# A sixth place for raw weights, paid for with the scratch tiles of an MLP's activation sums

## The chip, the cores and the metric

One NeuronCore of a Trainium2 chip runs the whole program. The metric is the device time of one execution in microseconds (us); a lower time is better. Times of a kernel are the median of several runs on a chip; one more execution is taken with the hardware profiler, and all spans, waits and busy times below come from that one.

## The reference

A two-layer decoder trunk on 256 tokens of width 2048, in float32. Layer 0 mixes tokens by differential attention, layer 1 by a Mamba-2 scan; after each mixer stands a squared-ReLU MLP, and it is the two MLPs that the change touches:

```
def sq_relu_mlp(h, w1, w2):
    return jnp.square(jax.nn.relu(h @ w1)) @ w2

for i in range(2):
    h = h + mixer_i(rms_norm(h, mixer_norm[i]))
    h = h + sq_relu_mlp(rms_norm(h, mlp_norm[i]), mlp_w1[i], mlp_w2[i])
```

`w1` is 2048 x 8192, `w2` is 8192 x 2048. Every weight is used once.

## The kernel before, in words

**Weights.** All weights stream from HBM in units of 128 x 1024 float32 (512 KB). A unit is loaded by the queue of SP (line 186) into a tile named `raw`; five places in SBUF hold such tiles in turn, and all stages share them. ScalarE (ACT) then rounds the unit to the fast matmul format (line 158), VectorE (DVE) subtracts to get the rest (line 159), and TensorE (PE) multiplies with both halves. The two halves make a `w` tile, of which there are four. So a unit passes through SP, ACT, DVE and PE, and a place of `raw` is free again when ACT and DVE have read it. SP issues its loads strictly in order: a load whose place is still in use holds up all loads behind it.

**Attention and Mamba stages** use `wide_pair` (lines 169 and 173) and `token_block` (lines 238 and 240): about 2.7 us of matmuls for each unit.

**The MLP.** The hidden width of 8192 is made in eight chunks of 1024. `MLP_KINDS = "sSSSSSSS"`: chunk 0 is made plainly (`blocks`, by `wide_steps`), the others by `seven`, a Strassen-like scheme with seven products of half-size blocks in place of eight. It needs sums of weights, which DVE makes: lines 569, 579, 584 and 600, each on 128 x 1024. It also needs sums of activations: `sum_parts` makes them eight times at the head of each MLP, from two pairs of activation tiles each time. One call is two additions into a tile `a` (line 530), four half-width additions into a tile `asum` (lines 534 to 537), a rounding by ACT (line 540) and a subtraction by DVE (line 541) into `sa`, which the products read. `a` and `asum` are scratch: they share a pair of 2 KB places of their own (tag `relu`) in the MLP's pool.

**Order.** The kernel is Python code that issues instructions; `side` holds generators that are ticked between matmuls, among them `norm_input` (activations of the next stage) and `sums_of` (which calls `sum_parts`). A tile scheduler then settles the order on each engine and which place a tile gets: a tile that finds no free place of its tag is delayed, and other instructions go first. Afterwards each engine runs its list strictly in order.

At the head of an MLP four things meet: the last residual additions of the mixer (line 319, in four pairs, each after a block of PE), the new activations (lines 273 and 274), the eight calls of `sum_parts`, and the first weights. The first two chunks are interleaved (`both(0, 28 / 12)`), so the first `seven` begins while chunk 0 is under way.

Of the kernel before, what the change touches and what calls it, by code (L numbers as in the profile page):

```python
# [12 lines left out]
F32 = mybir.dt.float32  # L13
# [7 lines left out]
P = 128  # L21
T = 256
# [69 lines left out]
def trunk_kernel(ctx: ExitStack, tc: tile.TileContext, x, xt, par, rope, qk, wv, wo, w10, w10s, w20, win, wdt, wout, w11, w11s, w21, out):  # L92
# [5 lines left out]
    wp = ctx.enter_context(tc.tile_pool(name="wp", bufs=1))  # L98
# [81 lines left out]

    def load(src, n=1):

        raw = wp.tile([P, 1024], F32, tag="raw", bufs=5, name="raw")
        w = 1024 // n
        for i in range(n):
            nc.sync.dma_start(out=raw[:, i * w:(i + 1) * w], in_=src[:, i * w:(i + 1) * w])
        return raw
# [4 lines left out]
    def wide_pair(src, b, acts):  # L192

        pp = [bank() for _ in range(2)]
        for s in range(2):
            raw = [load(src[b + t, s]) for t in range(2)]
            w = [split_weights(raw[t]) for t in range(2)]
            for i in range(2):
                for t in range(2):
                    sub_part(w[t], acts, 8 * s, pp[t], i, s == 0, s == 1)  # L200
        return pp

    def wide_steps(src, b, acts, dst):

        pp = bank()
        for s in range(2):
            sub_block(split_weights(load(src[b, s])), acts, 8 * s, pp, s == 0, s == 1)
            yield
        add_sums(dst, [pp])

    def wide_one(src, b, acts):
        pp = bank()
        raw = [load(src[b, s]) for s in range(2)]
        for s in range(2):
            sub_block(split_weights(raw[s]), acts, 8 * s, pp, s == 0, s == 1)
        return pp
# [51 lines left out]
    def x_parts(src, j, gain):  # L268

        t, parts = act_pair()  # L270
        for i in range(2):
            g = pa[:, gain + 2 * j + i:gain + 2 * j + i + 1]
            S.activation(t[:, i, 0, :], src[:, i, :], AF.Identity, scale=g)
            V.scalar_tensor_tensor(out=t[:, i, 1, :], in0=src[:, i, :], scalar=g, in1=t[:, i, 0, :].bitcast(F32),
                                   op0=ALU.mult, op1=ALU.subtract)
        return parts
# [48 lines left out]
    with tc.tile_pool(name="xin", bufs=1) as xp:  # L325
        raw, xf = [], []
        for s in range(2):
            pool = (wp, xp)[s]
            raw.append([pool.tile([P, 1024], F32, tag="raw", bufs=(5, 4)[s], name="raw") for _ in range(4)])
        for g in range(4):  # L330
            for j in range(2):
                xf.append(xp.tile([P, 2, T], F32, tag="xf", bufs=8, name="xf"))
                nc.sync.dma_start(out=xf[-1], in_=x[2 * g + j])
                if j == 0:
                    for b in range(4):
                        c = slice(512 * (g % 2), 512 * (g % 2 + 1))
                        nc.sync.dma_start(out=raw[g // 2][b][:, c], in_=qk[b, g // 2][:, c])
        w = None
        for g in range(4):
            if g % 2 == 0:  # L340
                w = [wp.tile([P, 2, 1024], F32R, tag="w", bufs=4, name="w") for _ in range(4)]
            for j in range(2):
                xs += x_parts(xf[2 * g + j], 2 * g + j, C_MIX0)
            for b in range(4):
                c = slice(512 * (g % 2), 512 * (g % 2 + 1))
                src = raw[g // 2][b][:, c]
                S.copy(out=w[b][:, 0, c], in_=src)
                V.tensor_tensor(out=w[b][:, 1, c], in0=src, in1=w[b][:, 0, c].bitcast(F32), op=ALU.subtract)
                for i in range(2):
                    for k in range(4):  # L350
                        kk = slice(512 * (g % 2) + k * P, 512 * (g % 2) + (k + 1) * P)
                        act = xs[4 * g + k]
                        if i == 0:
                            PE.matmul(first[b], lhsT=w[b][:, 0, kk], rhs=act, start=(g + k == 0), stop=False)
                        else:
                            PE.matmul(first[b][:, 0, :], lhsT=w[b][:, 1, kk], rhs=act[:, 0, :], start=False, stop=(g + k == 6))
# [168 lines left out]

    def sum_parts(pool, x, dst):

        a = pool.tile([P, 2, T], F32, tag="relu", bufs=2, name="a")
        for i in range(2):
            V.tensor_tensor(out=a[:, i, :], in0=x[i][:, 0, :].bitcast(F32), in1=x[i][:, 1, :].bitcast(F32), op=ALU.add)  # L530
        a11, a21, a12, a22 = (a[:, i, t * P:(t + 1) * P] for i in range(2) for t in range(2))
        f = pool.tile([P, 4, P], F32, tag="relu", bufs=2, name="asum")
        yield
        V.tensor_tensor(out=f[:, 0, :], in0=a21, in1=a22, op=ALU.add)
        V.tensor_tensor(out=f[:, 1, :], in0=f[:, 0, :], in1=a11, op=ALU.subtract)
        V.tensor_tensor(out=f[:, 2, :], in0=a11, in1=a21, op=ALU.subtract)
        V.tensor_tensor(out=f[:, 3, :], in0=a12, in1=f[:, 1, :], op=ALU.subtract)
        yield
        sa = pool.tile([P, 2, 4, P], F32R, tag="sa", bufs=8, name="sa")
        S.copy(out=sa[:, 0], in_=f)  # L540
        V.tensor_tensor(out=sa[:, 1], in0=f, in1=sa[:, 0].bitcast(F32), op=ALU.subtract)
        x0, x1 = x
        s1, s2, s3, s4 = ([sa[:, i, n, :] for i in range(2)] for n in range(4))
        dst.append([[x0[:, i, 0:P] for i in range(2)], s4, [x1[:, i, 0:P] for i in range(2)], s1, s3, s2, [x1[:, i, P:T] for i in range(2)]])
        yield
# [64 lines left out]
    def mlp(xs, w1, w1s, w2, pool, after):  # L610
# [3 lines left out]
        def sums_of():  # L614
            for j in range(KT // 2):
                while len(xs) < 2 * j + 2:
                    yield
                yield from sum_parts(pool, xs[2 * j:2 * j + 2], sas)
# [458 lines left out]
```

## Time and profile before

| what | value |
|---|---|
| median of 3 runs | 2450.47 us (2450.01 to 2451.3) |
| the profiled execution | 2449.62 us, its span 2447.9 us |
| PE busy | 2434.1 us, 99% of the span |
| PE weight loads busy | 2038.8 us, 83% |
| DVE busy | 2098.2 us, 86% |
| ACT busy | 1535.6 us, 63% |
| read from HBM | 496.24 MB, 204 GB/s over the span |
| attention | 0 to about 380 us |
| MLP of layer 0 | about 380 to 1070 us |
| Mamba | about 1070 to 1740 us |
| MLP of layer 1 | about 1740 to 2448 us |

The page of the profile lists busy times by engine, the span in 40 slices, the chain of work that ended last, and groups of instructions by source line. The trace gives waits by who ended them, busy times within a stretch, and instructions in order of time; there a bracket such as `[1.31 <-DMA raw]` is idle time of the engine just before the instruction and what ended it. Ends of matmuls are modelled, so PE's busy time is not a measure of how well it is used.

### The profile page before, as it was taken

Reading aid. Unit: us, or ns where it says so; the run is one execution under the profiler, and the core shown is the slowest. Engines: PE = TensorE matmul, PEld = TensorE weight load, DVE = VectorE, ACT = ScalarE, POOL = GpSimd, SP = SyncE. Lnnn points to the kernel's source line nnn. Section 1 sums busy time; section 2 is a strip of 40 time slices with the busy share of each in tenths; the row PEclk is TensorE's granted clock in tenths of the full one; section 3 lists DMA queues with packets and bytes.
Section 4 is the critical chain, followed back from the end, with each engine's and each line's share of the span. In section 5 each row is a group of like instructions: output and inputs, shape, how many; then the busy total and the mean of one; then the engine's idle time right before and its main releaser. Section 6 shows DMA issues by size and latency. Waiting matters only on the chain.

```text
span 2447.9 us, 32626 instructions
## 1 busy us (share of the span) xinstructions
PE 2434.1 (99%) x12050; PEld 2038.8 (83%) x12050; DVE 2098.2 (86%) x2591; ACT 1535.6 (63%) x2154; POOL 1.2 (0%) x8
## 2 busy tenths in 40 slices
PE   9999999999999999999999999999999999999999
PEld 8888888878888788888888888888887888878887
DVE  6988879999998999568886887887899999899964
ACT  7666656666666666456776575775666666666653
POOL 0000000000000000000000000000000000000000
PEclk9999999999999999999999999999999999999999
DMA  8545555667667676556565556556566766776764
GB/s 287 164 157 175 167 175 194 208 232 243 230 208 230 221 231 218 191 177 211 190 198 196 174 198 199 166 189 191 190 218 220 239 229 203 238 232 206 233 205 147
DMA packets 140192, 500.54 MB, mean 204 GB/s; under 512 B 15648, under 2 KB 15840, under 8 KB 140032
## 3 DMA queue, kind: packets, MB, share of 16 engines
q1 hardware_dynamic: 137312, 489.75, 61.3%
q10 hardware_dynamic: 2720, 8.71, 1.0%
q8 instruction: 94, 1.54, 0.2%
q14 instruction: 66, 0.54, 0.1%
HBM read 496.24 MB, written 2.16 MB: 204 GB/s over the span
## 4 chain that ended last, share of the span: by engine, by line
PE 70%; DVE 18%; DMA 7%; issue 4%; ACT 1%; DVEq 0%; SPq 0%; ACTq 0%
PE pp L238 21%; PE pp L169 16%; DVE w L159 11%; PE pp L240 10%; PE pp L173 9%; PE aux L557 6%; DMA raw<-in_w11s 3%; DMA raw<-in_w10s 3%; PE aux L559 3%; DVE wsum L569 1%; DVE wsum L600 1%; DVE raw L579 1%; PE aux L878 1%; DVE h L716 1%; ACT w L158 1%
## 5 line engine op out<-in xcount | busy, mean ns | idle before, releaser
L159 DVE TENSOR_TENSOR w<-raw,w 128x1024 fp32r<-128x1024 f32 x858 | 1034.6, 1219 | 196.1 <-ACT w L158 193.5
L158 ACT CAST w<-raw 128x1024 fp32r<-128x1024 f32 x858 | 892.7, 1052 | 493.4 <-PE pp L238 316.3
L238 PE MATMUL pp<-w,act 128*128 128x512 f32 x3072 | 983.1, 391 | 0.7 <-ACT w L158 0.7
L238 PEld LDWEIGHTS pp<-w,act 128*128 128x128 f32 x3072 | 575.4, 188 | 121.7 <-ACT w L158 1.5
L240 PE MATMUL pp<-w,act 128*128 128x512 f32 x1536 | 598.5, 390 | 0.0
L169 PE MATMUL pp<-act,w 128*128 128x512 f32 x2000 | 489.0, 392 | 0.0
L169 PEld LDWEIGHTS pp<-act,w 128*128 128x128 f32 x2000 | 366.4, 188 | 72.6 <-issue 1.0
L240 PEld LDWEIGHTS pp<-w,act 128*128 128x128 f32 x1536 | 288.3, 188 | 58.0
L557 PE MATMUL aux<-w,sa 128*128 128x512 f32 x896 | 300.3, 392 | 5.2 <-DVE act L264 1.7
L173 PEld LDWEIGHTS pp<-act,w 128*128 128x128 f32 x2000 | 258.3, 191 | 11.0 <-issue 0.9
L173 PE MATMUL pp<-act,w 128*128 128x256 f32 x2000 | 266.8, 284 | 0.0
L158 ACT CAST w<-wsum 128x1024 fp32r<-128x1024 f32 x168 | 176.9, 1053 | 114.6 <-PE pp L238 43.8
L557 PE MATMUL aux<-w,act 128*128 128x512 f32 x672 | 228.8, 394 | 0.8 <-ACT w L158 0.3
L159 DVE TENSOR_TENSOR w<-wsum,w 128x1024 fp32r<-128x1024 f32 x168 | 204.8, 1219 | 1.9 <-ACT w L158 1.5
L557 PEld LDWEIGHTS aux<-w,sa 128*128 128x128 f32 x896 | 167.4, 188 | 44.3 <-DVE w L159 4.7
L559 PE MATMUL aux<-w,sa 128*128 128x512 f32 x448 | 175.2, 391 | 0.0
L557 PEld LDWEIGHTS aux<-w,act 128*128 128x128 f32 x672 | 124.8, 188 | 32.2 <-DVE w L159 6.2
L559 PE MATMUL aux<-w,act 128*128 128x512 f32 x336 | 131.4, 391 | 0.0
L559 PEld LDWEIGHTS aux<-w,sa 128*128 128x128 f32 x448 | 84.2, 188 | 16.7
L569 DVE TENSOR_TENSOR wsum<-raw 128x1024 f32<-128x1024 f32 x56 | 68.4, 1222 | 21.4 <-DMA raw<-in_w10s 11.5
L579 DVE TENSOR_TENSOR raw<-raw 128x1024 f32<-128x1024 f32 x56 | 68.5, 1222 | 20.4 <-DMA raw<-in_w11s 11.4
L600 DVE TENSOR_TENSOR wsum<-wsum,raw 128x1024 f32<-128x1024 f32 x56 | 68.0, 1220 | 7.4 <-DMA raw<-in_w11s 3.9
(218 smaller groups left out, 1736.0 us busy)
## 6 DMA issues: line engine op xcount, KB each, us to landing
raw<-in_w SPq DMA_DIRECT2D x288, 512.0 KB, 4.4
raw<-in_win SPq DMA_DIRECT2D x160, 512.0 KB, 4.1
raw<-in_w10s SPq DMA_DIRECT2D x140, 512.0 KB, 4.3
raw<-in_w11s SPq DMA_DIRECT2D x140, 512.0 KB, 4.3
raw<-in_wout SPq DMA_DIRECT2D x64, 512.0 KB, 4.1
raw<-in_qk SPq DMA_DIRECT2D x56, 512.0 KB, 4.3
raw<-in_wv SPq DMA_DIRECT2D x32, 512.0 KB, 4.2
raw<-in_wo SPq DMA_DIRECT2D x32, 512.0 KB, 4.2
```

Of the source, the lines that this page charges most:

```text
L158: S.copy(out=wh[:, s], in_=raw[:, s])
L159: V.tensor_tensor(out=wl[:, s], in0=raw[:, s], in1=wh[:, s].bitcast(F32), op=ALU.subtract)
L169: PE.matmul(acc, lhsT=wk, rhs=acts[k0 + k], start=(start and k == 0), stop=False)
L173: PE.matmul(acc[:, 0, :], lhsT=wk, rhs=acts[k0 + k][:, 0, :], start=False, stop=(stop and k == 7))
L238: PE.matmul(pp[t], lhsT=act[:, 0, tok], rhs=m, start=(s + i + k == 0), stop=(s == n - 1 and i + k == 2))
L240: PE.matmul(pp[t], lhsT=act[:, 1, tok], rhs=m, start=False, stop=False)
L557: PE.matmul(pp, lhsT=ah, rhs=m, start=(i + kp + j == 0), stop=(i == 3 and kp + j == 2))
L559: PE.matmul(pp, lhsT=al, rhs=m, start=False, stop=False)
L569: V.tensor_tensor(out=a[i], in0=b11, in1=b12, op=ALU.subtract)
L579: V.tensor_tensor(out=b12, in0=b22, in1=b12, op=ALU.subtract)
L600: V.tensor_tensor(out=a[i], in0=a[i], in1=b21, op=ALU.subtract)
L716: V.scalar_tensor_tensor(out=h[:, t, cols(j)], in0=pp[t], scalar=r2[:, t:t + 1], in1=h[:, t, cols(j)], op0=ALU.mult, op1=ALU.add)
```

## The change

`raw` gets six places instead of five, in the two spots that name the number. The scratch tiles `a` and `asum` of `sum_parts` no longer have places of their own: each takes a whole place of `raw` and uses the first half of it. In SBUF this is even: one more place of 4 KB, less two of 2 KB.

```
-        raw = wp.tile([P, 1024], F32, tag="raw", bufs=5, name="raw")
+        raw = wp.tile([P, 1024], F32, tag="raw", bufs=6, name="raw")
...
-            raw.append([pool.tile([P, 1024], F32, tag="raw", bufs=(5, 4)[s], name="raw") for _ in range(4)])
+            raw.append([pool.tile([P, 1024], F32, tag="raw", bufs=(6, 4)[s], name="raw") for _ in range(4)])
...
     def sum_parts(pool, x, dst):
-        a = pool.tile([P, 2, T], F32, tag="relu", bufs=2, name="a")
+        a = wp.tile([P, 1024], F32, tag="raw", bufs=6, name="a")[:, 0:2 * T].rearrange("p (a b) -> p a b", a=2)
...
-        f = pool.tile([P, 4, P], F32, tag="relu", bufs=2, name="asum")
+        f = wp.tile([P, 1024], F32, tag="raw", bufs=6, name="asum")[:, 0:4 * P].rearrange("p (a b) -> p a b", a=4)
```

No instruction is added or removed on any engine. SP's list of loads is the same but for one store of the output near the end. The lists of PE, ACT and DVE are the same up to the head of the first MLP and in the Mamba stage, and differ within the MLPs. Three places on DVE show how.

First, DVE at the second pair of residual additions at the head of the first MLP (`h` is the residual, `act` an activation tile, `w<-raw` the split of a weight unit). Before, from the first activations on:

```order
L530 TENSOR_TENSOR a<-act 128x256
L274 SCALAR_TENSOR_TENSOR act<-aux,pa,act 128x256 x2
L530 TENSOR_TENSOR a<-act 128x256
L536 TENSOR_TENSOR asum<-a 128x128
L159 TENSOR_TENSOR w<-raw,w 128x1024
L534 TENSOR_TENSOR asum<-a 128x128
L535 TENSOR_TENSOR asum<-asum,a 128x128
L537 TENSOR_TENSOR asum<-a,asum 128x128
L530 TENSOR_TENSOR a<-act 128x256 x2
L159 TENSOR_TENSOR w<-raw,w 128x1024
L541 TENSOR_TENSOR sa<-asum,sa 128x512
L319 TENSOR_TENSOR h<-pp,h 128x512 x2
```

The same stretch now, up to the first sum and a little beyond:

```order
L274 SCALAR_TENSOR_TENSOR act<-aux,pa,act 128x256 x4
L159 TENSOR_TENSOR w<-raw,w 128x1024 x2
L319 TENSOR_TENSOR h<-pp,h 128x512 x2
L159 TENSOR_TENSOR w<-raw,w 128x1024
L530 TENSOR_TENSOR a<-act 128x256 x2
L159 TENSOR_TENSOR w<-raw,w 128x1024
L274 SCALAR_TENSOR_TENSOR act<-aux,pa,act 128x256 x2
L534 TENSOR_TENSOR asum<-a 128x128
```

The first sum and the beginning of the second moved behind the pair of residual additions. Counted the same way, before the third pair stood three whole sums, now one whole sum and more than half of the second; before the fourth pair stood five, now three whole ones, more than half of the fourth and one addition of the fifth.

Second, DVE where the third and fourth subtraction of weights (line 569) of the first `seven` stand. Before:

```order
L569 TENSOR_TENSOR wsum<-raw 128x1024
L159 TENSOR_TENSOR w<-raw,w 128x1024
L159 TENSOR_TENSOR w<-wsum,w 128x1024
L159 TENSOR_TENSOR w<-raw,w 128x1024
L537 TENSOR_TENSOR asum<-a,asum 128x128
L569 TENSOR_TENSOR wsum<-raw 128x1024
L222 TENSOR_TENSOR u<-pp,u 128x256
L541 TENSOR_TENSOR sa<-asum,sa 128x512
L530 TENSOR_TENSOR a<-act 128x256 x2
```

Now:

```order
L159 TENSOR_TENSOR w<-raw,w 128x1024 x2
L569 TENSOR_TENSOR wsum<-raw 128x1024
L535 TENSOR_TENSOR asum<-asum,a 128x128
L536 TENSOR_TENSOR asum<-a 128x128
L537 TENSOR_TENSOR asum<-a,asum 128x128
L569 TENSOR_TENSOR wsum<-raw 128x1024
L159 TENSOR_TENSOR w<-wsum,w 128x1024
L541 TENSOR_TENSOR sa<-asum,sa 128x512
L159 TENSOR_TENSOR w<-raw,w 128x1024 x2
```

Between the two subtractions stand three small additions now, where three splits of weights stood. The eighth and last sum, whose first two additions close the first fence, now ends two rows behind the last subtraction.

Third, DVE at the end of the first `seven` (lines 603 and 604 finish it) and the beginning of the second. Before:

```order
L569 TENSOR_TENSOR wsum<-raw 128x1024
L603 TENSOR_TENSOR u<-aux,u 128x512
L604 TENSOR_TENSOR u<-u,aux 128x512
L264 TENSOR_TENSOR act<-u,act 128x2x256
L159 TENSOR_TENSOR w<-wsum,w 128x1024
```

Now:

```order
L603 TENSOR_TENSOR u<-aux,u 128x512
L604 TENSOR_TENSOR u<-u,aux 128x512
L569 TENSOR_TENSOR wsum<-raw 128x1024
L264 TENSOR_TENSOR act<-u,act 128x2x256
L569 TENSOR_TENSOR wsum<-raw 128x1024
L159 TENSOR_TENSOR w<-wsum,w 128x1024
```

The finishing additions moved ahead of a subtraction, and a second subtraction moved ahead of the split of `wsum`.

On PE the units stand in the same order; at some of them a few matmuls of two neighbouring units are now interleaved. By the places that the scheduler gave out, four of the six hold `a` or `asum` tiles at one point of the head of each MLP, around the fifth and sixth sum; two are then left for weights.

## The prediction

> **What bounds the kernel now.** I read the page first, for the engine shares and the clock.
>
> ```profile
> span 2447.9 us, 32626 instructions
> PE 2434.1 (99%) x12050; PEld 2038.8 (83%) x12050; DVE 2098.2 (86%) x2591; ACT 1535.6 (63%) x2154; POOL 1.2 (0%) x8
> PEclk9999999999999999999999999999999999999999
> PE 70%; DVE 18%; DMA 7%; issue 4%; ACT 1%; DVEq 0%; SPq 0%; ACTq 0%
> L159 DVE TENSOR_TENSOR w<-raw,w 128x1024 fp32r<-128x1024 f32 x858 | 1034.6, 1219 | 196.1 <-ACT w L158 193.5
> L569 DVE TENSOR_TENSOR wsum<-raw 128x1024 f32<-128x1024 f32 x56 | 68.4, 1222 | 21.4 <-DMA raw<-in_w10s 11.5
> raw<-in_w10s SPq DMA_DIRECT2D x140, 512.0 KB, 4.3
> ```
>
> PE is busy for 99% at full clock, and the chain is mostly PE, so PE is the bound. A modelled end can hide a short wait, so I take the distance of matmuls in a stretch without waits from the instructions in order of time:
>
> ```profile
> 1002.61 1.29 PE L238 MATMUL pp<-w,act 128*128 128x512 f32 x5
> 1003.74 0.39 PE L240 MATMUL pp<-w,act 128*128 128x512 f32 x1
> ```
>
> Five matmuls of 512 columns start within 1003.74 - 1002.61 = 1.13 us, one each 0.226 us, though one is shown as 0.39 long. So about 0.16 us of a wait is invisible as idle time. Next, the busy times by stretch: the head of each MLP in two parts, and the rest of its `seven` chunks (after the stretch the columns are its length, then PE, PEld, DVE, ACT).
>
> ```profile
> 380.00:430.00 50.00, 50.00 (x260) 42.70 (x259) 47.03 (x85) 34.88 (x56) 0.00 (x0) 1.00 0.60 194
> 430.00:500.00 70.00, 68.64 (x335) 56.52 (x335) 69.99 (x79) 50.29 (x64) 0.00 (x0) 1.00 0.66 215
> 500.00:960.00 460.00, 458.05 (x2044) 375.99 (x2043) 432.77 (x413) 289.00 (x314) 0.00 (x0) 1.00 0.69 227
> 1738.00:1788.00 50.00, 50.00 (x260) 42.68 (x259) 47.06 (x85) 35.06 (x56) 0.00 (x0) 1.00 0.62 200
> 1788.00:1860.00 72.00, 69.25 (x340) 57.09 (x339) 70.59 (x80) 49.45 (x63) 0.00 (x0) 1.00 0.64 207
> 1860.00:2320.00 460.00, 458.68 (x2043) 375.82 (x2042) 432.60 (x413) 290.12 (x316) 0.00 (x0) 1.00 0.69 227
> ```
>
> PE's idle time in these is 1.36 + 1.95 + 2.75 + 1.32 = 7.4 us: that is what better supply could return, plus the invisible part. And in the second part of the head DVE, not PE, has no time left: 69.99 of 70 us. A microsecond that DVE loses ahead of it can't be made up there. The waits of the whole span tell who waits for whom:
>
> ```profile
> ACT w L158 <- PE pp L238: 360.2, 245, 3.0
> DVE wsum L569 <- DMA raw<-in_w10s: 11.5, 11, 2.9
> DVE raw L579 <- DMA raw<-in_w11s: 11.4, 14, 1.7
> PEld aux L557 <- DVE w L159: 10.9, 27, 1.9
> SPq L186 <- DVE w L159: 1641.8, 751, 11.7
> ```
>
> SP waits nearly always for DVE to free a place of `raw`, so the ring of five is what paces loads; but ACT waits 360 us for PE to free a `w` tile: mostly the units are ready early and the ring costs nothing. PE feels DVE only in the products of `seven`, 27 times in 10.9 us (weight loads, which run ahead of matmuls).
>
> **The change part by part.** Work is neither added nor taken away, so every term is a wait that comes or goes.
>
> *A sixth place outside the MLPs.* Each load there may start one unit earlier, but units already wait for PE (the 360 us above). Nothing; without that cover a load's 4.3 us would show.
>
> *The sums start later.* One call of `sum_parts` on DVE:
>
> ```profile
> L530 DVE TENSOR_TENSOR a<-act 128x256 f32<-128x256 f32 x32 | 12.6, 418 | 0.1
> L534 DVE TENSOR_TENSOR asum<-a 128x128 f32<-128x128 f32 x16 | 4.6, 285 | 0.0
> L541 DVE TENSOR_TENSOR sa<-asum,sa 128x512 fp32r<-128x512 f32 x16 | 11.0, 685 | 0.0
> ```
>
> 2 x 0.418 + 4 x 0.285 + 0.685 = 2.66 us, or 21 us for the eight. The old scratch was always there; now a sum needs two places that weights hold. By the order, ahead of the second, third and fourth pair of residual additions stand 3.5, 3.6 and 3.2 us less of sums than before (one sum and two additions of line 530, 2.66 + 0.84, at the second). These pairs wait for blocks of PE, and the splits between them for a free `w` tile, so DVE, now 47.03 of 50 us busy, idles there instead. The work is done later, next to the first products. DVE may use part of the spare time by splitting early where a `w` tile happens to be free. So DVE comes 0.9 to 3.5 us late into the stretch in which it has no time; I take 2.5, nearer to the upper end, as DVE was held by `w` tiles for most of that time.
>
> *Raw waits at the head.* Before, three of the subtractions of line 569 wait for their loads:
>
> ```profile
> 412.39 1.23 DVE L569 TENSOR_TENSOR wsum<-raw 128x1024 f32<-128x1024 f32 x1 [0.51 <-DMA raw<-in_w10s]
> 420.38 1.23 DVE L569 TENSOR_TENSOR wsum<-raw 128x1024 f32<-128x1024 f32 x1 [0.81 <-DMA raw<-in_w10s]
> 426.30 1.22 DVE L569 TENSOR_TENSOR wsum<-raw 128x1024 f32<-128x1024 f32 x1 [1.08 <-DMA raw<-in_w10s]
> 1800.53 1.23 DVE L579 TENSOR_TENSOR raw<-raw 128x1024 f32<-128x1024 f32 x1 [1.41 <-DMA raw<-in_w11s]
> ```
>
> That is 2.40 us. From the freeing of the place to the use DVE had 4.2, 4.2 and 3.9 us of work, and with the waits some 5.0 us passed. Now, by the order, 4.7, 5.1 and 3.3 us lie between (the last: a split, a subtraction and three small additions, 1.22 + 1.22 + 0.86), so 0.3, 0 and 1.7 us of waiting stay. If a load takes its median 4.3, 0, 0 and 1.0 stay. Saved: 0.4 to 1.4; I take the middle, 0.9.
>
> *Order where PE and DVE tie.* Two places of the first MLP, PE beside DVE:
>
> ```profile
> 437.27 1.22 DVE L159 TENSOR_TENSOR w<-raw,w 128x1024 fp32r<-128x1024 f32 x1
> 438.90 0.62 PE L557 MATMUL aux<-w,sa 128*128 128x512 f32 x2
> 490.19 0.51 PE L557 MATMUL aux<-w,sa 128*128 128x512 f32 x1 [0.76 <-DVE u L604]
> 490.72 1.22 DVE L159 TENSOR_TENSOR w<-wsum,w 128x1024 fp32r<-128x1024 f32 x1
> 491.99 0.73 PE L557 MATMUL aux<-w,sa 128*128 128x512 f32 x2
> ```
>
> At the first, the split ends at 438.49, 0.4 us before PE needs it. Now a whole further sum (with other rows 2.8 us) stands ahead of it: PE waits up to 2.8 - 0.4 = 2.4 us there. At the second, the split ends at 491.94 and PE starts 0.05 us later; now one more subtraction (1.22) and one line 264 addition (0.69) stand ahead of it, and two matmuls (0.45) more ahead on PE: 1.4 us. A wait at the first only hides waits that follow, so the later tie settles the sum: DVE's lateness plus 1.4.
>
> First MLP's head: 2.5 - 0.9 + 1.4 = +3.0 us. (From about 0 to 4.5: with 0.9 late, 1.4 saved and the tie 1.4 less the 0.76 wait for line 604, which is done earlier now, nearly 0; with 3.5, 0.4 and 1.4, 4.5.) Second MLP's head: the same order, but its 1.41 us wait at 1800.53 goes, since 6.6 us of DVE work now lie ahead of that use where 4.1 did: +1.6.
>
> *The rest of the `seven` chunks.* The largest waits of PE that follow:
>
> ```profile
> 826.72 1.23 DVE L569 TENSOR_TENSOR wsum<-raw 128x1024 f32<-128x1024 f32 x1 [1.31 <-DMA raw<-in_w10s]
> 831.05 0.50 PE L557 MATMUL aux<-w,sa 128*128 128x512 f32 x1 [1.19 <-DVE act L264]
> 1802.94 0.50 PE L557 MATMUL aux<-w,sa 128*128 128x512 f32 x1 [1.45 <-DVE w L159]
> 2184.82 1.23 DVE L569 TENSOR_TENSOR wsum<-raw 128x1024 f32<-128x1024 f32 x1 [0.64 <-DMA raw<-in_w11s]
> 2189.15 0.51 PE L557 MATMUL aux<-w,sa 128*128 128x512 f32 x1 [0.54 <-DVE act L264]
> ```
>
> At 826.72 and 2184.82 the place is free 5.0 us of DVE work ahead of the use now, 3.7 before, so up to 1.2 + 0.5 us of PE's waits could go. But elsewhere the new order spends the place at once: DVE's subtractions moved ahead by one split, and as many loads as before (30 against 28 in the first MLP) have under 4.5 us of DVE work between freeing and use; the one before 826.72 now has 2.4 where it had 5.0. I take -0.6, a third of the 1.7, between -3 (all of PE's 1.95 + 1.32) and +2.
>
> The Trainium skill speaks for the change here: "Perfetto Trace Analysis", section "Optimization Strategy", says that consistent bubbles on the engine that should be saturated can mean too little SBUF for the next tile, buffer counts included. By that rule this term would be -3.3 and the heads would not pay. The trace agrees only in part: the bubbles are few, not consistent, and DVE's lack of time makes those of the head. Rival 1 below is where this rule would lead.
>
> Sum: 3.0 + 1.6 - 0.6 = +4.0 us on the profiled execution, 2449.6 to 2453.6. The median of the runs, 2450.47, lies 0.85 above the profiled execution, so the forecast is 2454 us (2454.5, cut to a whole number).
>
> **Rivals.** A measurement of this kernel can tell about 0.2%, 4.9 us, from no change.
>
> 1. *The ring helps the products.* Loads arrive a place earlier wherever DVE or PE waited. For it: SP's 1641.8 us behind DVE. Against: DVE's subtractions moved forward as well. PE would get back 7.4 us seen idle and up to 27 x 0.16 = 4.3 us unseen: 2439 to 2445, at best. It decides when both heads cost nothing and over 5 us of the 11.7 return.
> 2. *The heads break even.* DVE uses the idle time for early splits and its raw waits vanish: two heads between -2 and +1, the rest -1: 2447.5 to 2450.5.
> 3. *The sums choke the ring.* With four of six places held by sums, two are left for weights, fewer than the five of before, and SP's list is in order, so one held place delays all. Then nothing of the 3.5 us is recovered, the third subtraction waits the full 1.7 us and the following splits once more: 3.5 + 1.7 + 1.4 = 6.6 at the first head, 5.2 at the second: 2462. It decides from 3.4 us a head on. "TensorE: Matmul & The Clock Gate" of the Trainium skill, in its section "Why this matters for your kernels", adds that gaps of PE over some 3 us halve its clock; such a gap in one piece would make this rival worse by an estimated 1.7 us a head. No run here shows it: the longest wait in an MLP is 1.45 us and the clock stays full.
>
> **How the numbers follow.** My forecast (heads +1 to +4 each, the rest about even; 2450.5 to 2457) has a chance of 0.55, rival 1 0.07, rival 2 0.18, rival 3 0.20. Of the forecast's chance two thirds lie under 2455.4, the 0.2% limit, with its upper terms above. So faster by over 0.2%: 0.07. Slower: 0.20 + 0.18 = 0.38. Within: 0.55. The range leaves out rival 1 and the far end of rival 3: 2448 to 2460.
>
> **What would show it.** Right: DVE busy for less than 46 of the 50 us from 380 to 430; a wait of PE for line 159 of 2 to 4 us near 440 and again near 1795; line 604's wait at 490 gone; the sum of waits for raw at line 569 hardly smaller; attention and Mamba the same to 1 us. Wrong: DVE as busy as before at the head (the scheduler's places come free earlier than I think), or a PE idle time after 500 near zero, would make the kernel faster than I say; several raw waits of over 2 us on DVE near 430 would make it slower.

## Result and profile after

| | time | against before |
|---|---|---|
| before | 2450.89 us (2450.01 to 2451.48, 4 runs) | |
| after | 2494.79 us (2487.62 to 2497.96, 4 runs) | 1.0175, interval 1.0153 to 1.0198 |

The forecast was 2454 us, 2448 to 2460. The kernel is 44 us slower. The profiled execution of the changed kernel is its fastest, 2487.62 us; its span is 2485.9 us, 38.0 over that of before. (Of all executions told here one stands apart: one of nine of the kernel of experiment 5 took 9739 us, and the median there, 2441.68 us, hardly moves without it.) The same lines of its page as were read of before:

```profile
span 2485.9 us, 32595 instructions
PE 2446.7 (98%) x12050; PEld 2041.5 (82%) x12050; DVE 2099.2 (84%) x2591; ACT 1538.2 (62%) x2154; POOL 1.2 (0%) x8
PE 70%; DVE 16%; DMA 9%; issue 3%; ACT 1%; DVEq 0%; ACTq 0%; SPq 0%
L569 DVE TENSOR_TENSOR wsum<-raw 128x1024 f32<-128x1024 f32 x56 | 68.3, 1223 | 41.9 <-DMA raw<-in_w11s 21.0
raw<-in_w10s SPq DMA_DIRECT2D x140, 512.0 KB, 4.4
```

No engine has more work: DVE is busy for 2099.2 us (2098.2 before). Loads take as long as before, 4.4 us (4.3). But line 569 is idle for 41.9 us ahead of its instructions, where it was 21.4. Waits of the whole span say who waits for that:

```profile
DVE wsum L569 <- DMA raw<-in_w11s: 21.0, 14, 3.8
DVE wsum L569 <- DMA raw<-in_w10s: 20.8, 13, 3.5
DVE raw L579 <- DMA raw<-in_w10s: 14.4, 13, 2.0
PEld aux L557 <- DVE w L159: 29.3, 42, 2.7
PE aux L557 <- DVE w L159: 13.4, 19, 2.3
PE aux L557 <- DVE act L264: 11.0, 4, 3.9
PE aux L557 <- ACT w L158: 7.0, 7, 2.1
```

DVE waits twice as long for raw units at line 569 (11.5 and 9.9 before), and PE now waits 13.4 us for the splits of line 159, where it lost 1.8 us, and 11.0 us for line 264 of DVE, in four waits of up to 3.9 us, where it lost 1.7 us in two.

**Where the 38 us are.** PE issues the units in the same order in both kernels (a few matmuls of neighbouring units apart), so the start of the matmul with the same number tells how far one kernel lies behind the other. How much PE falls behind the kernel before in each stage (worked out from the starts of the 12050 matmuls; experiments, told below, in the lower rows):

| kernel | attention | head of MLP 0 (380 to 500) | rest of MLP 0 | Mamba | head of MLP 1 (1745 to 1870) | rest of MLP 1 | sum |
|---|---|---|---|---|---|---|---|
| after | -0.4 | +5.1 | +14.0 | 0.0 | +3.3 | +16.1 | +38.0 |
| six places, own scratch | -0.7 | +2.1 | +10.9 | 0.0 | +0.3 | +16.3 | +28.9 |
| five places, shared | +0.6 | +12.5 | -0.1 | 0.0 | +9.8 | +2.7 | +25.5 |
| after, old order | +0.1 | +6.3 | -3.8 | 0.0 | +7.2 | -4.3 | +5.5 |
| before, new order | -0.7 | 0.0 | +108.5 | 0.0 | +0.9 | +107.6 | +216.4 |
| six, own scratch, old order | +1.2 | +1.3 | -4.0 | 0.0 | -0.4 | -4.3 | -6.1 |
| after, four places mended | +1.5 | +8.8 | +0.5 | 0.0 | +7.0 | +5.0 | +22.8 |
| after, rule of four | -0.3 | +4.1 | -3.9 | 0.0 | +5.9 | -3.7 | +2.0 |
| six, own scratch, rule of four | -0.8 | +1.3 | -3.7 | 0.0 | -0.4 | -3.7 | -7.3 |
| before, rule of four | +0.1 | -1.7 | -2.2 | 0.0 | -3.2 | -2.8 | -9.8 |

So the heads cost 8.4 us, and 30 us are lost in the rest of the `seven` chunks, which the forecast had held to be about even. Of these 30, four places hold 22: near 660, 829, 2018 and 2189 us of the kernel before, where one `seven` chunk has ended, its hidden activations are transposed and split (lines 656 and 264), and the next chunk's sums of weights begin. First DVE in the kernel before, at the first of them (start, length, instruction, and in brackets the idle time ahead of it):

```profile
656.21 1.41 DVE L716 SCALAR_TENSOR_TENSOR h<-pp,r,h 128x512 f32<-128x512 f32 x2 [0.18 <-PE pp L238]
657.53 1.22 DVE L159 TENSOR_TENSOR w<-raw,w 128x1024 fp32r<-128x1024 f32 x1
658.66 1.22 DVE L569 TENSOR_TENSOR wsum<-raw 128x1024 f32<-128x1024 f32 x1
659.80 1.28 DVE L264 TENSOR_TENSOR act<-aux,act 128x512 fp32r<-128x512 f32 x2
```

Then DVE at the same place in the changed kernel:

```profile
656.63 1.22 DVE L569 TENSOR_TENSOR wsum<-raw 128x1024 f32<-128x1024 f32 x1
657.76 1.22 DVE L159 TENSOR_TENSOR w<-raw,w 128x1024 fp32r<-128x1024 f32 x1
658.90 1.22 DVE L159 TENSOR_TENSOR w<-wsum,w 128x1024 fp32r<-128x1024 f32 x1
663.65 1.23 DVE L569 TENSOR_TENSOR wsum<-raw 128x1024 f32<-128x1024 f32 x1 [3.54 <-DMA raw<-in_w10s]
664.80 1.22 DVE L159 TENSOR_TENSOR w<-raw,w 128x1024 fp32r<-128x1024 f32 x1
665.93 1.41 DVE L716 SCALAR_TENSOR_TENSOR h<-pp,r,h 128x512 f32<-128x512 f32 x2
667.25 1.22 DVE L159 TENSOR_TENSOR w<-raw,w 128x1024 fp32r<-128x1024 f32 x1
668.38 1.28 DVE L264 TENSOR_TENSOR act<-aux,act 128x512 fp32r<-128x512 f32 x2
```

And PE, with what it waits for:

```profile
666.07 0.73 PE L557 MATMUL aux<-w,act 128*128 128x512 f32 x2 [1.77 <-DVE w L159]
669.12 0.79 PE L557 MATMUL aux<-w,sa 128*128 128x512 f32 x1 [1.87 <-DVE act L264]
669.72 0.63 PE L559 MATMUL aux<-w,sa 128*128 128x512 f32 x1
670.14 0.63 PE L557 MATMUL aux<-w,sa 128*128 128x512 f32 x1
```

The second subtraction of line 569 in these rows stands ahead of two splits of raw units and of line 716 now; line 264 stood behind it already. The place that its load needs came free at 657.85, when the subtraction before it ended; two splits later DVE is there, but the load, issued with three others still under way, lands 5.7 us after the freeing. DVE stands still for 3.54 us, and everything behind it is late. Of that, the split is what PE needs next (1.77 us), and line 264 is what frees the `aux` bank (memory for PE's sums) that PE writes next (1.87 us). In the kernel before, this subtraction (at 658.66) stood behind those splits and its load was there.

The last two PE rows show a second loss: matmuls that start 0.42 us apart, where 0.226 us was the rule. The granted clock (seventh column) by windows of 3.41 us around it, in the changed kernel:

```profile
661.88:665.30 3.42, 2.41 (x15) 1.76 (x13) 1.65 (x2) 2.35 (x4) 0.00 (x0) 1.00 0.56 229
665.30:668.71 3.41, 1.19 (x4) 0.67 (x4) 3.41 (x5) 1.05 (x1) 0.00 (x0) 1.00 0.72 221
668.71:672.12 3.41, 3.00 (x8) 2.31 (x9) 3.23 (x4) 0.03 (x1) 0.00 (x0) 0.50 0.80 237
672.12:675.53 3.41, 3.41 (x19) 2.82 (x17) 2.36 (x3) 2.10 (x3) 0.00 (x0) 1.00 0.50 171
```

PE is busy for 1.19 of 3.41 us in the second window, and gets half its clock in the third. In all the clock is at half for 20.5 us within the MLPs, after each of the four waits; matmuls that start in these stretches are spaced 6.6 us wider in sum than at full clock. So of the 38 us some 31 are waits and some 7 the clock.

### The profile page after: what moved, and what is told of

Same layout as the page of the kernel before. It is cut to its first block, busy times and chain, and to the rows that moved or that the text cites. A ratio compares the mean times of both kernels' runs of the same rounds, so it can differ in the third digit from the quotient of the medians.

```text
span 2485.9 us, 32595 instructions
## 1 busy us (share of the span) xinstructions
PE 2446.7 (98%) x12050; PEld 2041.5 (82%) x12050; DVE 2099.2 (84%) x2591; ACT 1538.2 (62%) x2154; POOL 1.2 (0%) x8
## 4 chain that ended last, share of the span: by engine, by line
PE 70%; DVE 16%; DMA 9%; issue 3%; ACT 1%; DVEq 0%; ACTq 0%; SPq 0%
PE pp L238 19%; PE pp L169 17%; PE pp L240 10%; DVE w L159 9%; PE pp L173 9%; PE aux L557 7%; DMA raw<-in_w10s 5%; DMA raw<-in_w11s 4%; PE aux L559 3%; PE aux L656 1%; DVE wsum L569 1%; DVE wsum L584 1%; DVE wsum L600 1%; PE aux L878 1%; DVE h L716 1%
## 5 line engine op out<-in xcount | busy, mean ns | idle before, releaser
L557 PE MATMUL aux<-w,sa 128*128 128x512 f32 x896 | 306.6, 399 | 23.7 <-DVE act L264 11.0
L559 PE MATMUL aux<-w,sa 128*128 128x512 f32 x448 | 177.5, 396 | 0.0
L569 DVE TENSOR_TENSOR wsum<-raw 128x1024 f32<-128x1024 f32 x56 | 68.3, 1223 | 41.9 <-DMA raw<-in_w11s 21.0
```

What stands on the lines that cost most here:

```text
L557: PE.matmul(pp, lhsT=ah, rhs=m, start=(i + kp + j == 0), stop=(i == 3 and kp + j == 2))
L559: PE.matmul(pp, lhsT=al, rhs=m, start=False, stop=False)
L569: V.tensor_tensor(out=a[i], in0=b11, in1=b12, op=ALU.subtract)
```

## The experiments

Times of before are those taken beside each group: 2448.0, 2448.1 and 2450.8 us. The theory: **six places change the order** that the scheduler writes, since its own account of time lets a load start one place earlier and so a weight sum be ready earlier than it is on the chip; it then puts the sum ahead of work that PE needs. (The order that it writes can be read in the traces; its account of time can't, so that half of the theory stays an argument.) The rivals: **the heads** (sums of activations hold raw places, and the rest follows), and **the place itself** (more loads in flight).

**1. Six places alone.** The sums are made in place in one 2 KB tile of their own, with no more instructions than before:

```
-        a = wp.tile([P, 1024], F32, tag="raw", bufs=6, ...)
+        a = pool.tile([P, 2, T], F32, tag="relu", bufs=1, name="a")
...
-        f = wp.tile([P, 1024], F32, tag="raw", bufs=6, ...)
+        f = a.rearrange("p a (b c) -> p (a b) c", b=2)
```

> Six places for raw, but the sums take none of them: each sum works in one 2 KB place of its own, in place. Order theory (six places make the scheduler put DVE's weight subtractions earlier, ahead of work that PE waits for, outside the heads too; the sums don't matter): 2482 to 2496 us, with the changed kernel's waits of PE near 664, 841, 2041 and 2218. Head theory (sums that hold raw places choke the loads and the rest follows from that): 2446 to 2452. Place theory (a sixth load in flight makes each load slower, whatever the order): 2482 to 2496.

2484.75 us, 1.0154 (1.0137 to 1.0171). The heads cost 2.4 us together, the rest 27.2: the loss outside the heads needs no sums in the ring. The head theory falls for that part. Of the heads' 8.4 us, 6.0 go with the sums.

**2. Sums in the ring, five places.** Only the second half of the change.

> Five places for raw, with the sums made in them: the other half of the change alone. Order theory: 2451 to 2457, the heads' cost only, since the order outside the heads is that of five places. Head theory: 2490 or more, as fewer places are left for weights than in the changed kernel. Place theory: 2451 to 2457.

2471.93 us, 1.0099 (1.0084 to 1.0114). This is neither 2451 to 2457 nor 2490. The order of the rest is that of five places (but for 52 rows of DVE's list), and the rest costs 2.6 us; but the heads cost 22.3. The reason is the third rival of the prediction: the ring is choked and PE stands still in one piece. The waits at the first head:

```profile
ACT w L158 <- DMA raw<-in_w: 4.6, 1, 4.6
```

PE in order of time:

```profile
441.98 3.68 PE L169 MATMUL pp<-act,w 128*128 128x512 f32 x8 [3.51 <-ACT w L158]
```

ACT waits 4.6 us for one load, and PE 3.51 us for ACT. So sums in the ring do cost at the head, with five places 12.5 and 9.8 us, with six 5.1 and 3.3.

**3. Six places with the old order, and five with the new.** The order of DVE, ACT and PE after each head is pinned with edges that order issue and wait for nothing; the table holds the numbers of the instructions as the other kernel issues them.

```
+def pin(tc):
+    traced = {i.name: i for i in tc.nc.cur_bb.bb.instructions}
+    for table in ORDERS:
...
+            tc.add_manual_dep(traced[name], last, mybir.DependencyInfo(mybir.DependencyClass.NoSync, ...))
```

> The changed kernel with the order of DVE, ACT and PE after each MLP's head pinned to that of the kernel before; heads, places and sums as in the changed kernel. Order theory: 2448 to 2458 (heads +6, and the sixth place may give a little back with the old order). Head theory: 2480 to 2496, nothing at the heads is different. Place theory: 2480 to 2496.

> The kernel before (five places, sums in their own scratch) with the order of DVE, ACT and PE after each MLP's head pinned to that of the changed kernel. Order theory: 2480 to 2515, at least the 32 us that the changed kernel loses outside the heads, and more if loads that start a place later make the waits longer. Head theory and place theory: 2449 to 2453.

After with the old order: 2455.53 us, 1.0029 (1.0018 to 1.0041). Before with the new order: 2662.58 us, 1.0880 (1.0863 to 1.0896). This settles it: the changed kernel loses its 30 us with the order and wins 8.1 us in the rest without it (-3.8 and -4.3, the place's worth at the old order). The new order is wrong by far with five places, since it counts on loads that start one place earlier. MLP 0 in the waits of the two kernels (lines are 132 higher in their files, so 701 is line 569), first after with the old order, then before with the new:

```profile
DVE wsum L701 <- DMA raw<-in_w10s: 2.2, 2, 1.7
```

The other:

```profile
DVE wsum L701 <- DMA raw<-in_w10s: 46.5, 21, 4.5
PE aux L689 <- DVE w L291: 60.5, 28, 4.5
```

Place and heads, as theories of the 30 us, both said 2480 or more for the first and no change for the second. The heads of the first cost 13.5 us here, 5.1 more than in the changed kernel: in its profiled run the clock is at half for three windows of 3.41 us at the heads, in that of the changed kernel for none.

**4. A part of the order.** In the changed kernel, DVE alone gets its old order at the four places, 24 and 21 rows in each MLP.

> The changed kernel with the old order of DVE pinned at four places only, 24 and 21 rows in each MLP, around the first weight sums of the second and third seven-product chunk that follow an expansion of hidden activations. At these places the changed kernel's matmuls fall 5.2, 5.2, 6.5 and 5.3 us further behind those of the kernel before, 22 of its 38 us. Order theory, with few places that matter: 22 us less than the changed kernel, 2468 to 2476. If the loss belongs to the order as a whole and moves to the next place when one is mended: 2484 or more.

2470.06 us, 1.0072 (1.0057 to 1.0087): 24.7 us less than the changed kernel, from 90 of DVE's 2591 instructions. The rest of the MLPs falls from 30.1 to 5.5 us behind. A few places hold the loss. (Its heads cost 15.8 us, with four windows at half clock.)

**5. Old order and own scratch together.** The table of experiment 3 in the kernel of experiment 1.

> Six places, each sum in one 2 KB place of its own, and the order of DVE, ACT and PE after each MLP's head pinned to that of the kernel before. Order theory, from the two runs that each have half of this: the heads as in the kernel with six places and own scratch (PE's lost time 4.7 and 1.8 us where the kernel before has 2.9 and 4.4), the rest as in the kernel with the old order (6.8 us where the kernel before has 12.9), so 6.8 us less than before: 2438 to 2446 us. If the old order only helps because the heads of the changed kernel are late anyway: 2448 to 2460.

2441.68 us, 0.9973 (0.9963 to 0.9984), 6.4 us less than before: the two halves add as worked out.

**6. A rule in the source instead of a table: order of the program.** The four kinds of weight sums may not be issued ahead of anything that the program wrote before them on DVE, with three kernels: the changed one, six places with own scratch, and before.

```
-            V.tensor_tensor(out=a[i], in0=b11, in1=b12, op=ALU.subtract)
+            tc.keep_in_program_order(V.tensor_tensor(out=a[i], in0=b11, in1=b12, op=ALU.subtract))
...
```

> The changed kernel with one edit: the four kinds of weight sums on DVE are issued in the order of the program. Order theory: 2448 to 2460, the waits outside the heads gone and the heads' cost left. If the order at the heads gets better by it too, 2444 to 2448. Head theory: 2480 or more.

> Six places, each sum in one 2 KB place of its own, and the four kinds of weight sums on DVE (lines 569, 579, 584, 600) issued behind all that the program wrote before them on DVE, instead of as early as the scheduler thinks their loads are there. Order theory: no such sum stands ahead of its load's arrival any more, so DVE's waits for raw loads inside the MLPs fall under 5 us in all and the time is 2438 to 2448. If instead the sums come too late for their own products, PE waits for line 159 and the time is 2452 or more.

> The kernel before with one edit: the same four kinds of weight sums issued in the order of the program; five places, own scratch. Order theory: part of the 12.9 us that PE loses outside the heads comes back, 2440 to 2450. If the sixth place is what gives the time back and not the order, 2449 to 2453.

2611.49, 2610.92 and 2610.05 us, 1.066 each: a miss for the order theory in all three. Only the other branch of the second (sums too late for their own products, 2452 or more) has the kind of loss, and not its size. DVE's raw waits are gone, but now a sum stands right before its own split in many places, with ACT's cast between them. The waits of the changed kernel with this rule, in its first MLP:

```profile
DVE w L159 <- ACT w L158: 106.0, 106, 1.5
PE aux L557 <- ACT w L158: 46.4, 41, 1.6
```

DVE waits for that cast 106 times, a microsecond each. The changed kernel falls 35 us behind at the heads and 128 in the rest. Too late costs more here than too early did (163 us against 44), and the number of places makes no difference.

**7. A rule between the two.** A weight sum is issued behind the split of the unit four units back (there are four `w` tiles), and otherwise as early as the scheduler likes. Again three kernels.

```
+            last_split.append(V.tensor_tensor(out=wl[:, s], ...))
...
+            with tc.issue_after(last_split[-4].ins):
+                V.tensor_tensor(out=a[i], in0=b11, in1=b12, op=ALU.subtract)
```

> The changed kernel with one rule in its source: each weight sum on DVE (lines 569, 579, 584, 600) is issued behind the split of the unit four units back. In the resulting order all but a few sums have over 4.4 us of DVE work between the freeing of their place and their use, and all but 4 have at least one other split between themselves and their own split. Order theory: neither raw waits nor waits for ACT's cast, so the heads' cost alone stays: 2448 to 2460. If any rule that holds sums back makes products late as the order of the program did: 2470 or more.

> The same rule, with six places and each sum of activations in one 2 KB place of its own. Order theory: 2438 to 2446, as the kernel with the pinned old order and own scratch (2441.7). If that kernel's gain is a matter of its particular order: 2448 or more.

> The same rule in the kernel before (five places, own scratch). Five places leave 29 us less room over one MLP's loads under 4.4 us than six (sum of what is missing to 4.4 us: 14.7 against 0.7 us), where the kernel before has 26.2 us missing. Order theory with the place as what the order can spend: between the kernel before and the six places, 2443 to 2452. If the place is worth nothing by itself: the same as six places with the rule.

After: 2449.96 us, 0.9999 (0.9990 to 1.0008). Six places with own scratch: 2443.25 us, 0.9971 (0.9959 to 0.9982). Before: 2440.70 us, 0.9960 (0.9946 to 0.9973), the fastest of the three, with five places, and below what was expected. (Against before it also does better than experiment 5, 0.9973, but the intervals overlap.) (The expectation of five places should say 28 us and not 29: 14.0 for each of two MLPs.) In the changed kernel the rule takes the rest from +30.1 to -7.6 us and leaves 10.0 at the heads. That five places would do better than six I had not expected: in the rest they get 5.0 us back, six get 7.4; but at the heads they get 4.9, where six places with a single scratch tile lose 0.9 and with sums in the ring 10.0. Why the heads gain with five places, no run shows.

```profile
span 2438.1 us, 32650 instructions
PE 2429.5 (100%) x12050; PEld 2039.2 (84%) x12050; DVE 2099.3 (86%) x2591; ACT 1531.1 (63%) x2154; POOL 1.2 (0%) x8
```

## Why the prediction was wrong, point by point

- *Nothing outside the MLPs*: right. Attention -0.4, Mamba 0.0 us.
- *Heads +3.0 and +1.6*: right in sign, too small; measured 5.1 and 3.3. That they came as near is luck, for the parts came out differently. The sums' later start was to leave DVE idle ahead of 430; it is busier there than before (47.92 of 50 us, 47.03 before; the prediction had named that as a sign of a faster kernel), and idle behind it, where it had no time to lose:

```profile
380.00:430.00 50.00, 48.71 (x250) 40.96 (x249) 47.92 (x97) 33.07 (x54) 0.00 (x0) 1.00 0.45 147
430.00:500.00 70.00, 65.92 (x320) 53.49 (x320) 67.44 (x70) 50.76 (x64) 0.00 (x0) 1.00 0.72 233
```

  The raw waits of line 569 were to save 0.9 us of their 2.40; they are 2.96 now, 1.27 of it at a subtraction that had not waited, and the last at its bound of 1.7:

```profile
413.30 1.23 DVE L569 TENSOR_TENSOR wsum<-raw 128x1024 f32<-128x1024 f32 x1 [1.27 <-DMA raw<-in_w10s]
...
433.41 1.23 DVE L569 TENSOR_TENSOR wsum<-raw 128x1024 f32<-128x1024 f32 x1 [1.69 <-DMA raw<-in_w10s]
```

  PE at the head, and at the second tie:

```profile
426.50 0.50 PE L557 MATMUL aux<-w,sa 128*128 128x512 f32 x1 [1.29 <-ACT w L158]
...
435.82 0.73 PE L557 MATMUL aux<-w,sa 128*128 128x512 f32 x2 [0.84 <-DVE w L159]
...
496.05 0.50 PE L557 MATMUL aux<-w,sa 128*128 128x512 f32 x1 [2.08 <-ACT w L158]
```

  PE's wait of 2 to 4 us for line 159 near 440 did not come (0.84), nor did that of the second head (0.54 at 1810.67). The second tie, near 490, did not settle the sum: PE waits 2.08 us there and line 604's wait is gone, but the kernel before lost time there too, and across the tie PE's lag grows only from 4.5 to 4.7 us. The loss had come between 425 and 440, where the lag goes from -0.4 to 4.8 us. Its first wait, 1.29 us at 426.50, is for the rounding of a weight sum that DVE makes at 424.15, before at 412.39; the later of its two loads was issued at 416.43 us, before at 408.36. The prediction's sum has no term for loads that start late because sums hold places; only its third rival has, and by experiment 1 the sums in the ring make 6.0 of the heads' 8.4 us.
- *The rest of the `seven` chunks, -0.6, between -3 and +2*: **this is the step that failed**: +14.0 and +16.1 us. Its gain rested on a row that was misread. It gave the subtractions at 826.72 and 2184.82 us 5.0 us of DVE work between the freeing of the place and the use. By the traces they have 3.7 us in both kernels, and now wait 2.06 us (1.31 before) and 2.35 us (0.64 before); the first of them now:

```profile
837.76 1.23 DVE L569 TENSOR_TENSOR wsum<-raw 128x1024 f32<-128x1024 f32 x1 [2.06 <-DMA raw<-in_w10s]
```

  The 5.0 us belong to the subtraction before that one, whose wait of 1.23 us is indeed gone, and the 2.4 us to the one before both, which now waits 2.35 us where it did not wait. The step also counted loads with little DVE work ahead of them, 30 against 28 under 4.5 us, and called that even. The traces show about the same (29 now, 32 before in the first MLP, of the loads that lines 569, 579 and 600 need last), but the count measures the wrong thing. A wait at the head of DVE's list costs what stands behind it, and at the four places that is a split that PE needs at once and the release of a bank. Elsewhere a wait can be free: in the kernel before, DVE waits 2.90 us at 744.05 for a load of line 569, and PE shows no idle time from 736 to 756. The step even noted that DVE's subtractions had moved ahead, and took this as an offset to a gain, not as a loss by itself. The sizes of the waits were missed too: 2.4 us of work ahead of a load of the median 4.3 us makes a wait of 1.9, and at 663.65 it was 3.54, since that load took 5.7 us. Loads issued in close sequence took as long in the kernel before (5.7 and 5.8 us for those of 649.78 and 650.93). The upper end of +2 had no row behind it: the nearest, 1.31 us at 826.72, was taken as if it were the largest, though the prediction's own list of waits has one of 2.9 us at line 569. And the sum has no term for the clock, 6.6 us.
- *Rival 1, the ring helps*: its mechanism is there, 8.1 us in the rest, as soon as the order is held; left to itself the scheduler spends the place on an order that loses 30. *Rival 3, the sums choke the ring*: true with five places (+22.3 us at the heads), and with six for 6.0 of the heads' 8.4 us.
- *The rule on the clock*: told with rival 3 as something that no run showed. The runs show it now, for shorter waits than 3 us and not at the heads alone: 6.6 us for four stretches at half clock, near the 1.7 us that were estimated for one.

## What to carry to other kernels

Where a scheduler writes the order, a buffer count is also an input to that order: compare the order first, and at each row that moved ahead ask what stands behind it on its in-order engine and how soon the bottleneck needs that, not only whether its own input is there. A place gained and an order lost can be told apart by pinning the order of one kernel on the other. Hold early work behind a point a few units back: an order made for six places and the strict order of the program cost far more here (+215 and +162 us at five places) than the sixth place gave (8 us). Four units back is the only distance that was tried.

## What the runs showed of the hardware

PE's clock goes to half after far shorter gaps than I had thought. In the ten of these runs that have such stretches ahead of the program's end, all of them begin on one grid of 3.413 us for each run, to within 4 ns (one run has a single stretch), and last one, two or three such windows (3.41, 6.83, 10.24 us). By PE's idle time within a window of that grid, while the clock is full:

| idle in the window | windows | next window at half clock |
|---|---|---|
| under 1.5 us | about 7100 | 0 |
| 1.5 to 1.9 us | 68 | 25 |
| over 1.9 us | 46 | 46 |

So about half a window of idle time is enough, in one piece or in several: before 668.71 the longest piece within the window was 1.45 us, the sum 2.23 us. (Ends of matmuls are modelled some 0.16 us late, as the prediction worked out, so each gap is longer than it looks.) The Trainium skill, "TensorE: Matmul & The Clock Gate", section "What's actually happening", tells of a free-running window of 4096 cycles, 3413 ns; the grid agrees with it. The same page of the Trainium skill, in its section "Why this matters for your kernels", asks for no idle gaps over some 3 us; here the measurement decides: gaps of 2 us that fall in one window do it. That the runs of the changed kernel range from 2487.62 us at a mean clock of 0.996 to 2497.96 at 0.994 would fit a grid that lies differently in each, but nothing here shows that.
